# The last head pair of a dilated-attention layer: its softmax shares spread by products, a quarter of its output kept on chip, more PSUM for the projection behind it

## Chip, cores and metric

One core of a Trainium2 chip runs the whole layer as one program. The metric is device time in microseconds (us) of that core, the median over runs of the same program.

## What is computed

The input x has 2048 tokens of 1024 floats. The layer is cut here to what matters:

```python
n = rmsnorm(x) ; proj = n @ w_in                 # split into a GLA group and an attention group
A = gla(...)                                     # 2048 x 512, gated linear attention
for (window, d) in ((128,1), (512,4), (2048,16)):# attention, 8 heads of 64: three branches
    s = masked(q k^T / 8) ; m = max(s) ; den = sum(exp(s - m)) ; o = exp(s - m) v / den
wts = den * exp(m - max over branches of m)
B = sum(wts * o) / sum(wts)                      # 2048 x 512, the branches combined per token and head
h = x + [A ; B] @ w_out
h = h + hier_moe(rmsnorm(h))                     # router: 4 groups of 8 experts, then 2 experts per token
y = rmsnorm(h)
```

A branch's weight over the sum of weights is its *share*; there are three per token and head.

## The kernel before, in words

All data are float32. A product that has to be exact is done as three products of a rounded part (`hi`, fp32r) and a remainder (`lo`): hi*hi, hi*lo, lo*hi. A tile framework puts in the waits, and a scheduler with a model of the engines' times sets the order of instructions on each engine; the source gives priorities by the order in which it emits, and `behind(a, b)` puts a after b.

The stages follow one another: `front` (norm and projection into all columns, with GLA woven in), `att` (lines 495 to 740), `mid` (lines 804 to 969: the attention half of the output projection, second norm, router), and the experts.

**Attention** goes over four pairs of heads, p = 0 to 3, in three branches of 16 query blocks each. `score`, `turn` and `weigh` are its steps, and the unnormalised output of a branch ends in a tile `o` of 128 rows (2 heads x 64) by 2048 tokens. `sums(p)` (line 602) turns the maxima and denominators, writes them to HBM (`stat`) and reads them back in another layout (`nd`, nine transfers, lines 612 to 618), 32 rows (head, block of 128 tokens) by 128 tokens. `shares(p)` (line 620) makes the three shares on VectorE (DVE) with one exponential on ScalarE (ACT), and writes them to HBM (`fac`, line 641). `combine(p, n, eng)` (line 643) handles a quarter n of the tokens, 512: two transfers read `fac` back, each row spread over the 64 rows of a head (`fb`, line 647), then come three multiplications (649), two additions (650, 651), and the result goes to HBM as rows of `oT` (652). For p < 3 all this lies behind the next pair's scores, with the arithmetic on GpSimd (POOL). For p = 3 nothing of attention is left to cover it.

**The GLA half of the output projection** is `out_gla` (line 742), a generator woven into attention: for each of 16 tiles of 128 tokens it turns the GLA output (`og`, line 757, PSUM tile `f`), and does two halves of 512 columns, twelve products each (777 to 779), in a PSUM tile `f` too. The pool `t_fps` has one buffer of that tile. DVE adds x (782), the sum goes to HBM as `hp` (783). `split_wout` (786) makes `hi` on ACT (799) and `lo` on DVE (800) of half the weights, 8 pieces; its second half is called by `mid`.

**mid** loads for each tile of 128 tokens the column block of `oT` (`ot`, 847) and `hp` (`h`, 849), splits `ot` (855, 856), does 24 products in PSUM tiles `mm` (867 to 869, a pool `m_mm` of three buffers), adds `h` (870), norms, and turns the result (894) for the router's products (913). Its products need all of `oT` for their tokens. At the end of the program's attention part, `steps()` runs `sums(3)`, frees the PSUM, sets up `mid`, finishes `out_gla`, makes the shares and combines quarter 0; `build` combines quarters 1 to 3 between mid's first tiles. The experts' weights are prefetched as of mid's third tile, and the experts start when the router's last tile is done.

Of the kernel before, what the change touches and what calls it, by code (L numbers as in the profile page):

```python
# [8 lines left out]
F32 = mybir.dt.float32  # L9
# [4 lines left out]
OP = mybir.AluOpType  # L14
# [3 lines left out]
T = 2048  # L18
# [38 lines left out]
class Layer:  # L57
    def __init__(self, tc, a, scratch):
        self.tc, self.nc, self.a = tc, tc.nc, a
        s = scratch  # L60
        self.gqT = s("gqT", (256, T))
        self.gkT = s("gkT", (256, T))

        self.aq, self.ak = (s(n, (512, T)) for n in ("aq", "ak"))
        self.gv = s("gv", (T, 512))
        self.gs = s("gs", (T, 512))
        self.av = s("av", (4, T, 128))
        self.la_d = s("la_d", (T, 256))
# [3 lines left out]
        self.fac = s("fac", (4, 3, 2 * T))  # L72
# [7 lines left out]
        self.last = None  # L80
        
# [413 lines left out]
    def att(self, gla, left):  # L495
# [83 lines left out]
        def weigh(p, br, blk, kbs, PT):  # L579
            g, b4 = divmod(blk, 4)  # L580
            if blk == 0:
                OU[p, br] = pools["on"].tile([128, T], F32, name=f"o{br}", bufs=2)
# [7 lines left out]
            if b4 == 3:  # L590
                O = OU[p, br]
# [10 lines left out]
        def sums(p):  # L602
# [17 lines left out]
        def shares(p):  # L620
# [19 lines left out]
            nc.vector.tensor_tensor(f[hi], f[hi], mn[hi].unsqueeze(1).broadcast_to((32, 3, 128)), OP.mult)  # L640
            nc.sync.dma_start(self.fac[p].rearrange("b (u m) -> u b m", m=128), f[hi])

        def combine(p, n, eng):
# [4 lines left out]
            for br in range(3):  # L648
                eng.tensor_tensor(fb[:, br], OU[p, br][:, c], fb[:, br], OP.mult)
# [4 lines left out]
        def steps():  # L654
# [81 lines left out]
        return right, lambda n: combine(3, n, nc.vector)  # L736


    def out_gla(self, pools, fps):
# [26 lines left out]
        for i in range(NT):  # L766
# [6 lines left out]
            for f in range(2):  # L773
                fs = slice(f * 512, (f + 1) * 512)
                pp = fps.tile([128, 512], F32, name="f")
                for k in range(4):
                    placed(0, nc.tensor.matmul(pp, oh[:, k, :], woh[:, k, fs], start=k == 0, stop=False))
                    nc.tensor.matmul(pp, oh[:, k, :], wol[:, k, fs], start=False, stop=False)
                    nc.tensor.matmul(pp, ol[:, k, :], woh[:, k, fs], start=False, stop=k == 3)
                    if k < 3:  # L780
                        yield 0.65
# [8 lines left out]
    def split_wout(self, keep, half, raws):  # L790
# [4 lines left out]
        for n in range(8):  # L795
# [4 lines left out]
            nc.vector.tensor_tensor(lo[:, k, c], raw, hi[:, k, c].bitcast(F32), OP.subtract)  # L800
# [5 lines left out]
    def mid(self, st):  # L806
# [6 lines left out]
        mm = pool("m_mm", 3, space=PSUM)  # L813
# [30 lines left out]
        def load(i):  # L844
            rows = slice(i * 128, (i + 1) * 128)
            ot = io.tile([128, 4, 128], F32, name="ot")
            nc.sync.dma_start(ot, self.oT[:, rows].rearrange("(k p) t -> p k t", p=128))
            h = io.tile([128, D], F32, name="h")
            self.loads.append(nc.sync.dma_start(h, self.hp[rows, :]))
            return ot, h  # L850

        def split(ot, h):
            oh = wk.tile([128, 4, 128], F32R, name="oh")
            ol = wk.tile([128, 4, 128], F32R, name="ol")
            nc.scalar.copy(oh, ot)
            nc.vector.tensor_tensor(ol, ot, oh.bitcast(F32), OP.subtract)
# [86 lines left out]
        for i in range(NT + 2):  # L943
            yield
            if i == 2:
# [516 lines left out]
def build(tc, a, scratch, start=None, stop=None):  # L1462
    L = Layer(tc, a, scratch)
    with tc.tile_pool(name="consts", bufs=1) as cp:
# [23 lines left out]
        for i, _ in enumerate(L.mids):  # L1488
            if i < 3:
                last(i + 1)  # L1490
            if i == 2:
# [30 lines left out]
```

## Time and profile before

| | us |
|---|---|
| median of 3 runs | 2243.97 (2239.78 to 2246.97) |
| the profiled execution, its own time | 2231.41 |
| its span, first to last instruction | 2229.7 |
| TensorE (PE) busy | 2080.5 (93%) |
| DVE busy | 1278.7 (57%) |
| ACT busy | 1059.4 (48%) |
| POOL busy | 453.3 (20%) |

The mean granted clock of TensorE is 0.965 of full speed. Engines run side by side, so the busy times add up to more than the span. Times in the rows below are us from the span's start. Attention's last product begins at 1109.11 us, the first product of mid (line 867) at 1154.85, the experts' first (line 1308) at 1328.66.

### The profile page before, as it was taken

Reading aid. Unit: us, or ns where it says so; the run is one execution under the profiler, and the core shown is the slowest. Engines: PE = TensorE matmul, PEld = TensorE weight load, DVE = VectorE, ACT = ScalarE, POOL = GpSimd, SP = SyncE. Lnnn points to the kernel's source line nnn. Section 1 sums busy time; section 2 is a strip of 40 time slices with the busy share of each in tenths; the row PEclk is TensorE's granted clock in tenths of the full one; section 3 lists DMA queues with packets and bytes.
Section 4 is the critical chain, followed back from the end, with each engine's and each line's share of the span. In section 5 each row is a group of like instructions: output and inputs, shape, how many; then the busy total and the mean of one; then the engine's idle time right before and its main releaser. Section 6 shows DMA issues by size and latency. Waiting matters only on the chain. (4 is left out here: it accounts for less than half of the span.)

```text
span 2229.7 us, 38492 instructions
## 1 busy us (share of the span) xinstructions
PE 2080.5 (93%) x15242; PEld 1566.4 (70%) x15242; DVE 1278.7 (57%) x2458; ACT 1059.4 (48%) x1805; POOL 453.3 (20%) x348
## 2 busy tenths in 40 slices
PE   7999999999997999999969978899999999999990
PEld 7799889799885766666647656567766766767760
DVE  5203336424435466666657775666767677767663
ACT  5412335523323366766713333455555555555542
POOL 2000000000002012352300252622212222222246
PEclk9999999999997999999989969999999999999995
DMA  8333333334316415453378727688888888878876
GB/s 252 110 123 101 113 123 110 110 105 128 110 62 202 165 67 143 142 137 95 94 213 297 255 93 251 235 288 302 300 296 283 301 308 312 299 274 291 312 262 235
DMA packets 191465, 440.30 MB, mean 197 GB/s; under 512 B 35201, under 2 KB 107298, under 8 KB 165410
## 3 DMA queue, kind: packets, MB, share of 16 engines
q1 hardware_dynamic: 141842, 351.40, 45.0%
q0 software_dynamic: 21488, 60.36, 10.3%
q10 hardware_dynamic: 27952, 26.05, 4.0%
q8 instruction: 121, 1.98, 0.4%
q14 instruction: 62, 0.51, 0.1%
HBM read 345.89 MB, written 92.40 MB: 197 GB/s over the span
## 5 line engine op out<-in xcount | busy, mean ns | idle before, releaser
L1258 DVE TENSOR_TENSOR lo<-raw,hi 128x2048 fp32r<-128x2048 f32 x192 | 439.4, 2290 | 128.3 <-ACT hi L1258 127.6
L1258 ACT CAST hi<-raw 128x2048 fp32r<-128x2048 f32 x192 | 365.3, 1905 | 208.6 <-DMA raw<-expert_w 195.5
L565 ACT ACTIVATE P<-P,st 128x256 f32<-128x256 f32 (+1 forms) x384 | 174.0, 455 | 96.7 <-DVE st L563 92.2
L214 PE MATMUL mm<-whi,nh 128*128 128x256 f32 x768 | 219.9, 286 | 0.0
L216 PE MATMUL mm<-whi,nl 128*128 128x256 f32 x768 | 218.1, 284 | 0.0
L215 PE MATMUL mm<-wlo,nh 128*128 128x256 f32 x768 | 217.6, 283 | 0.0
L1310 PE MATMUL mm<-lo,nh 128*128 128x512 f32 x512 | 206.8, 405 | 0.0
L1308 PE MATMUL mm<-hi,nh 128*128 128x512 f32 x512 | 204.6, 400 | 1.1 <-ACT nh L1286 1.1
L1309 PE MATMUL mm<-hi,nl 128*128 128x512 f32 x512 | 201.1, 393 | 0.0
L129 POOL TENSOR_TENSOR ss<-ss,mhalf 128x1 f32<-128x1 f32 (+3 forms) x40 | 34.6, 865 | 701.2 <-DVE ss L128 700.9
L563 DVE CUSTOM_DVE_ANT_0 P<-s,amask 128x256 f32<-128x256 f32 (+1 forms) x384 | 124.9, 362 | 66.1 <-PE s L559 42.9
L191 PE MATMUL mm<-nh,whi 128*128 128x512 f32 x384 | 154.5, 402 | 0.0
L192 PE MATMUL mm<-nl,whi 128*128 128x512 f32 x384 | 153.1, 399 | 0.0
L193 PE MATMUL mm<-nh,wlo 128*128 128x512 f32 x384 | 152.7, 398 | 0.0
L214 PEld LDWEIGHTS mm<-whi,nh 128*128 128x128 f32 x768 | 145.4, 189 | 2.0 <-issue 0.7
L215 PEld LDWEIGHTS mm<-wlo,nh 128*128 128x128 f32 x768 | 145.5, 189 | 0.8 <-DVE wlo L177 0.4
L216 PEld LDWEIGHTS mm<-whi,nl 128*128 128x128 f32 x768 | 144.8, 189 | 0.1
L1317 PE MATMUL r<-raw,nr 128*32 128x256 f32 x2048 | 142.9, 383 | 0.0
L559 PE MATMUL s<-k,q 64*128 64x256 f32 (+1 forms) x768 | 132.8, 416 | 0.2 <-DVE st L563 0.2
L1364 POOL DMA_INDIRECT acc<-y,it x32 | 88.7, 2771 | 212.6 <-ACT y L1361 204.9
L1310 PEld LDWEIGHTS mm<-lo,nh 128*128 128x128 f32 x512 | 96.6, 189 | 42.2 <-issue 20.6
L177 DVE TENSOR_TENSOR wlo<-raw,whi 128x1024 fp32r<-128x1024 f32 x48 | 57.0, 1222 | 112.7 <-ACT whi L176 112.7
(326 smaller groups left out, 4147.7 us busy)
## 6 DMA issues: line engine op xcount, KB each, us to landing
raw<-expert_w SPq DMA_DIRECT2D x192, 1024.0 KB, 10.6
raw<-w_in ACTq DMA_DIRECT2D x48, 512.0 KB, 4.9
fb<-fac SPq DMA_DIRECT2D x32, 384.0 KB, 8.4
x<-x SPq DMA_DIRECT2D x16, 512.0 KB, 4.8
og<-og SPq DMA_DIRECT2D x32, 256.0 KB, 4.4
xr<-x SPq DMA_DIRECT2D x32, 256.0 KB, 3.0
v<-av SPq DMA_DIRECT2D x8, 1024.0 KB, 8.1
hp<-xr SPq DMA_DIRECT2D x32, 256.0 KB, 2.3
```

The costliest lines, as they stand in the source:

```text
L191: nc.tensor.matmul(ps, hi[:, k, ms], nh[q][:, k, :], start=k == 0, stop=False)
L192: nc.tensor.matmul(ps, hi[:, k, ms], nl[q][:, k, :], start=False, stop=False)
L193: nc.tensor.matmul(ps, lo[:, k, ms], nh[q][:, k, :], start=False, stop=k == KD - 1)
L214: nc.tensor.matmul(ps[:, j, :], h, hi[:, k, :], start=j == 0 and k == 0, stop=False, skip_group_check=True)
L215: nc.tensor.matmul(ps[:, j, :], h, lo[:, k, :], start=False, stop=False, skip_group_check=True)
L216: nc.tensor.matmul(ps[:, j, :], l, hi[:, k, :], start=False, stop=k == KD - 1, skip_group_check=True)
L565: nc.scalar.activation(P[:, h, 0:w], P[:, h, 0:w], AF.Exp, bias=nm, scale=-1.0, accum_out=dn)
L1258: split = nc.scalar.copy(hi, raw), nc.vector.tensor_tensor(lo, raw, hi.bitcast(F32), OP.subtract)
L1308: nc.tensor.matmul(ps[m], nh[:, k, :], hi[:, kk, :], start=k == 0, stop=False)
L1309: nc.tensor.matmul(ps[m], nl[:, k, :], hi[:, kk, :], start=False, stop=False)
L1310: nc.tensor.matmul(ps[m], nh[:, k, :], lo[:, kk, :], start=False, stop=k == KD - 1)
L1317: nc.tensor.matmul(pr[32 * g:32 * g + 32], nr[:, k, :], raw[:, k % 4, (g % 2) * 256:(g % 2) * 256 + 256], start=k == 0, stop=k == KD - 1, ...
```

## The change

For the last pair only, the shares stay in SBUF (`self.f3`, 32 rows by 3 x 128), and `combine_last` takes the place of `combine`. For each block of 128 tokens two products of a column of the identity (spread to 32 x 64) with the shares copy one row of shares for each head to 64 rows of a PSUM tile of `mm`: 384 columns, plain f32. DVE multiplies the three branches by it straight from PSUM, one instruction of 128 x 384. So there are 2 products and 1 multiplication per block, 32 and 16 in all. The additions of quarter 0 are DVE's, those of quarters 1 to 3 POOL's. Quarter 0 is not written to `oT`: mid's tiles 0 to 3 read it from SBUF (`self.att3`), and split it apart from the other three pairs.

Beside it: the three branches' outputs share one tile; four of the nine `nd` transfers of the last pair are issued by ACT; `lo` of the second half of `w_out` is made on POOL; the second half of each remaining tile of `out_gla` uses a PSUM tile of `mm` once attention is over; `sums` and `shares` are emitted ahead of mid's setup, two tiles of `out_gla` ahead of the combination; quarters 2 and 3 are combined one tile of mid later, as are the experts' first pool and the router's.

```diff
             if b4 == 3:
-                O = OU[p, br]
+                O = OU[p][:, br]
...
+            second = nc.scalar if p == 3 else nc.sync
             for j in range(4):
-                nc.sync.dma_start(nd[j::4, 1].rearrange("g (q i) -> g q i", q=4), src[j])
+                second.dma_start(nd[j::4, 1].rearrange("g (q i) -> g q i", q=4), src[j])
...
+            if p == 3:
+                self.f3 = f
+                return
             nc.sync.dma_start(self.fac[p].rearrange("b (u m) -> u b m", m=128), f[hi])
+
+        def combine_last(n, eng):
+
+            c = slice(n * 512, (n + 1) * 512)
+            fb = pools["sm"].tile([128, 3, 512], F32, name="fb", bufs=2)
+            for b in range(4):
+                blk = 4 * n + b
+                ps = self.mmp.tile([128, 512], F32, name="mm")
+                for h in range(2):
+                    sel = self.ident[32:64, 32 + 16 * h + blk:33 + 16 * h + blk].broadcast_to((32, 64))
+                    mm = nc.tensor.matmul(ps[64 * h:64 * h + 64, 0:384], sel, self.f3[32:64].rearrange("u b m -> u (b m)"),
+                                          start=True, stop=True, skip_group_check=True)
+                    if n == 0:
+                        self.behind(mm, self.outlast, "the factors come later than these products")
+                nc.vector.tensor_tensor(fb[:, :, 128 * b:128 * b + 128], OU[3][:, :, 128 * blk:128 * blk + 128],
+                                        ps[:, 0:384].rearrange("p (b m) -> p b m", b=3), OP.mult)
+            eng.tensor_tensor(fb[:, 0], fb[:, 0], fb[:, 1], OP.add)
+            eng.tensor_tensor(fb[:, 0], fb[:, 0], fb[:, 2], OP.add)
+            if n == 0:
+                self.att3 = fb[:, 0]
+            else:
+                nc.sync.dma_start(self.oT[384:512, c], fb[:, 0])
...
             sums(3)
+            drain(shares(3))
             work.close()
             kst.close()
             self.mids = self.mid(left)
             next(self.mids)
+            weave(out, iter(()), 0, 2)
+            combine_last(0, nc.vector)
             drain(out)
-            sh = shares(3)
-            for _ in range(3):
-                next(sh, None)
-            combine(3, 0, nc.vector)
...
-                pp = fps.tile([128, 512], F32, name="f")
+                pp = fps.tile([128, 512], F32, name="f") if f == 0 or not self.mmp else self.mmp.tile([128, 512], F32, name="mm")
...
-            nc.vector.tensor_tensor(lo[:, k, c], raw, hi[:, k, c].bitcast(F32), OP.subtract)
+            (nc.gpsimd if half else nc.vector).tensor_tensor(lo[:, k, c], raw, hi[:, k, c].bitcast(F32), OP.subtract)
...
+            nk = 3 if i < 4 else 4
+            nc.sync.dma_start(ot[:, 0:nk], self.oT[0:128 * nk, rows].rearrange("(k p) t -> p k t", p=128))
...
+            if i < 4:
+                parts = [(slice(0, 3), ot[:, 0:3]), (slice(3, 4), self.att3[:, i * 128:(i + 1) * 128].unsqueeze(1))]
...
         for i, _ in enumerate(L.mids):
-            if i < 3:
-                last(i + 1)
-            if i == 2:
+
+            for n in {0: (1,), 3: (2, 3)}.get(i, ()):
+                last(n)
+            if i == 3:
                 right.close()
                 L.moe_raw()
```

What stands in a row on an engine changes at three places. Up to attention's last product the order is that of before. The first place is PE between attention and mid; before, the last products of `out_gla` that fall there (`f`) are followed by mid's first (867):

```order
L777 MATMUL f<-woh,oh 128x512
L778 MATMUL f<-wol,oh 128x512
L779 MATMUL f<-woh,ol 128x512
L867 MATMUL mm<-woh,oh 128x512
L868 MATMUL mm<-wol,oh 128x512
```

Of the change, the first of quarter 0's products (655) and, further on, the end of the stretch:

```order
L801 MATMUL f<-woh,oh 128x512
L802 MATMUL f<-wol,oh 128x512
L803 MATMUL f<-woh,ol 128x512
L655 MATMUL mm<-f,ident 64x384 x6
L781 MATMUL f<-ident,og 128x128 x4
L655 MATMUL mm<-f,ident 64x384 x2
L801 MATMUL mm<-woh,oh 128x512
```

Quarter 0 stands behind half a tile of `out_gla`, in the same row on PE. The end of the stretch, with quarter 1's last copies and mid's first products (897 to 899):

```order
L801 MATMUL mm<-woh,oh 128x512
L802 MATMUL mm<-wol,oh 128x512
L803 MATMUL mm<-woh,ol 128x512
L655 MATMUL mm<-f,ident 64x384 x4
L897 MATMUL mm<-woh,oh 128x512
```

Before, 72 of the 108 products of `out_gla` that attention left over stood ahead of mid's first product, and 36 among mid's first tiles. Now all 108 stand ahead, 48 of them before the first 655 rows and 60 behind, and so do 16 of the 32 copying products.

The second place is DVE, in the second half of the shares (638 to 640, `f` at the end is the shares). Before:

```order
L782 TENSOR_TENSOR xr<-f,xr 128x512
L638 TENSOR_TENSOR mn<-nd 32x128
L800 TENSOR_TENSOR wol<-xr,woh 128x512
L638 TENSOR_TENSOR mn<-mn,nd 32x128
L800 TENSOR_TENSOR wol<-xr,woh 128x512
L639 RECIPROCAL mn<-mn 32x128
L800 TENSOR_TENSOR wol<-xr,woh 128x512
L835 CAST tri<-trf 128x128
L761 TENSOR_TENSOR ol<-f,oh 128x512
L800 TENSOR_TENSOR wol<-xr,woh 128x512
L640 TENSOR_TENSOR f<-f,mn 32x384
```

Of the `lo` pieces of `w_out` (800) four stand among the shares. The same part of DVE's row in the change (785 and 806 are `out_gla`'s):

```order
L806 TENSOR_TENSOR xr<-mm,xr 128x512
L859 CAST tri<-trf 128x128
L638 TENSOR_TENSOR mn<-nd 32x128
L785 TENSOR_TENSOR ol<-f,oh 128x512
L638 TENSOR_TENSOR mn<-mn,nd 32x128
L639 RECIPROCAL mn<-mn 32x128
L640 TENSOR_TENSOR f<-f,mn 32x384
L806 TENSOR_TENSOR xr<-f,xr 128x512
L659 TENSOR_TENSOR fb<-o,mm 128x3x128 x4
```

They have left the row; all eight stand in a row on POOL now. Behind the shares come quarter 0's four multiplications (659), with no transfer between.

The third place is PE in mid, between the last product of tile 2 and the first of tile 3 (924 turns a tile for the router, 943 and 948 are the router's). Before, a tile's turning stood among products of the next tile, or of `out_gla`:

```order
L868 MATMUL mm<-wol,oh 128x512
L869 MATMUL mm<-woh,ol 128x512
L894 MATMUL tp<-ident,n_11426 128x128 x8
L867 MATMUL mm<-woh,oh 128x512
L868 MATMUL mm<-wol,oh 128x512
```

Nothing but a tile's turning parts the products there. Of the change, at the end of tile 2:

```order
L899 MATMUL mm<-woh,ol 128x512
L655 MATMUL mm<-f,ident 64x384 x2
L924 MATMUL tp<-ident,n_11435 128x128 x8
L655 MATMUL mm<-f,ident 64x384 x6
L943 MATMUL sm<-nT,rw 64x256 x8
L655 MATMUL mm<-f,ident 64x384 x2
L924 MATMUL tp<-ident,n_11497 128x128 x8
L655 MATMUL mm<-f,ident 64x384 x4
L948 MATMUL sm<-ident,lT 128x128 x2
L655 MATMUL mm<-f,ident 64x384 x2
L897 MATMUL mm<-woh,oh 128x512
```

Quarters 2 and 3 are copied here, 16 products in one place, and tile 2's own turning now stands ahead of tile 3's products.

## Rows read from the trace of the kernel before

**Rows 1.** Busy time by stretch: us, engines busy (instructions), clock share, DMA share, GB/s
```profile
1109.70:1154.85 45.15, 25.97 (x87) 18.90 (x85) 22.27 (x40) 8.20 (x14) 0.00 (x0) 0.77 0.69 201
1154.85:1301.40 146.55, 139.35 (x742) 106.53 (x740) 102.52 (x293) 49.89 (x123) 25.67 (x32) 0.98 0.80 256
```

**Rows 2.** Waits of PE, 1109 to 1180 us: total, times, longest
```profile
PE f L777 <- DVE ol L761: 11.9, 3, 6.5
PE f L777 <- DVE xr L782: 4.5, 3, 2.7
```

**Rows 3.** Timeline of PE: start, us, line, out<-in, count, idle before and releaser
```profile
1109.70 0.66 PE L757 MATMUL f<-ident,og 128*128 128x128 f32 x4
1111.76 0.50 PE L777 MATMUL f<-woh,oh 128*128 128x512 f32 x1 [1.40 <-DVE ol L761]
...
1125.42 0.79 PE L777 MATMUL f<-woh,oh 128*128 128x512 f32 x1 [4.04 <-DVE ol L761]
...
1130.27 0.44 PE L779 MATMUL f<-woh,ol 128*128 128x512 f32 x1
1131.59 0.47 PE L777 MATMUL f<-woh,oh 128*128 128x512 f32 x1 [0.88 <-DVE xr L782]
...
1134.17 0.39 PE L779 MATMUL f<-woh,ol 128*128 128x512 f32 x1
...
1142.47 0.80 PE L777 MATMUL f<-woh,oh 128*128 128x512 f32 x1 [6.47 <-DVE ol L761]
...
1154.85 0.40 PE L867 MATMUL mm<-woh,oh 128*128 128x512 f32 x1
```

**Rows 4.** Timeline of DVE, the shares and the first combination
```profile
1115.86 0.39 DVE L628 TENSOR_TENSOR mn<-nd 32x128 f32<-32x128 f32 x1 [0.29 <-DMA nd<-stat]
...
1121.11 0.69 DVE L800 TENSOR_TENSOR wol<-xr,woh 128x512 fp32r<-128x512 f32 x1
...
1125.99 0.55 DVE L640 TENSOR_TENSOR f<-f,mn 32x384 f32<-32x384 f32 x1
...
1139.91 1.90 DVE L649 TENSOR_TENSOR fb<-o,fb 128x512 f32<-128x512 f32 x3 [4.63 <-DMA fb<-fac]
...
1145.87 1.90 DVE L649 TENSOR_TENSOR fb<-o,fb 128x512 f32<-128x512 f32 x3 [2.86 <-DMA fb<-fac]
```

**Rows 5.** Timeline of SP's queue (issues), then of ACT
```profile
1109.61 0.33 SPq L609 DMA_DIRECT2D stat<-sb  x1
...
1114.48 2.06 SPq L618 DMA_DIRECT2D nd<-stat  x4
...
1132.01 1.92 SPq L647 DMA_DIRECT2D fb<-fac  x3
...
1150.52 0.37 SPq L847 DMA_DIRECT2D ot<-oT  x1
...
1153.69 0.62 ACT L855 CAST oh<-ot 128x512 fp32r<-128x512 f32 x1 [17.02 <-DMA ot<-oT]
```

**Rows 6.** Timeline of PE in mid: plain f32 products, then the next instruction
```profile
1293.36 1.95 PE L913 MATMUL sm<-nT,rw 128*64 128x256 f32 x16
1295.24 0.50 PE L869 MATMUL mm<-woh,ol 128*128 128x512 f32 x1
```

**Rows 7.** Instructions of lines 649 and 870: ns min/median/max, first and last start
```profile
L649 POOL TENSOR_TENSOR fb<-o,fb x36: 1261/1276/1301, 876.7 to 1079.2; 128x512 f32<-128x512 f32 x36
...
L649 DVE TENSOR_TENSOR fb<-o,fb x12: 684/686/693, 1139.9 to 1170.6; 128x512 f32<-128x512 f32 x12
...
L870 DVE TENSOR_TENSOR h<-mm,h x32: 680/686/709, 1163.8 to 1297.5; 128x512 f32<-128x512 f32 x32
```

**Rows 8.** Timelines of POOL and of DVE among the experts
```profile
1413.92 0.96 POOL L1186 DMA_INDIRECT perm<-tok,pos  x1 [0.30 <-issue]
1415.19 3.04 POOL L1186 DMA_INDIRECT perm<-tok,pos  x1 [0.30 <-issue]
...
1415.10 2.29 DVE L1258 TENSOR_TENSOR lo<-raw,hi 128x2048 fp32r<-128x2048 f32 x1 [1.48 <-ACT hi L1258]
```

**Rows 9.** Waits of PE, 1180 to 1300 us
```profile
PE mm L867 <- DVE h L870: 4.7, 1, 4.7
```

More of the change, by code (lines that the diff above doesn't have):

```diff
@@ L71, in __init__ @@
         self.stat = s("stat", (4, 192, 128))
-        self.fac = s("fac", (4, 3, 2 * T))
+        self.fac = s("fac", (3, 3, 2 * T))
         self.oT = s("oT", (512, T))
@@ L79, in __init__ @@
         self.entries, self.loads = [], []
-        self.last = None
+        self.last = self.mmp = None
     def pool(self, st, name, bufs, **k):
@@ L580, in weigh @@
             g, b4 = divmod(blk, 4)
-            if blk == 0:
-                OU[p, br] = pools["on"].tile([128, T], F32, name=f"o{br}", bufs=2)
+            if (br, blk) == (0, 0):
+                OU[p] = pools["on"].tile([128, 3, T], F32, name="o", bufs=2)
             if b4 == 0:
@@ L648, in combine @@
             for br in range(3):
-                eng.tensor_tensor(fb[:, br], OU[p, br][:, c], fb[:, br], OP.mult)
+                eng.tensor_tensor(fb[:, br], OU[p][:, br, c], fb[:, br], OP.mult)
             eng.tensor_tensor(fb[:, 0], fb[:, 0], fb[:, 1], OP.add)
@@ L735, in att @@
         drain(steps(), out)
-        return right, lambda n: combine(3, n, nc.vector)
+        return right, lambda n: combine_last(n, nc.gpsimd)
     def out_gla(self, pools, fps):
@@ L778, in out_gla @@
                     nc.tensor.matmul(pp, oh[:, k, :], wol[:, k, fs], start=False, stop=False)
-                    nc.tensor.matmul(pp, ol[:, k, :], woh[:, k, fs], start=False, stop=k == 3)
+                    self.outlast = nc.tensor.matmul(pp, ol[:, k, :], woh[:, k, fs], start=False, stop=k == 3)
                     if k < 3:
@@ L812, in mid @@
         wk = pool("m_wk", 2)
-        mm = pool("m_mm", 3, space=PSUM)
+        mm = self.mmp = pool("m_mm", 3, space=PSUM)
         tps = pool("m_tps", 2, space=PSUM)
@@ L846, in load, with split @@
             ot = io.tile([128, 4, 128], F32, name="ot")
-            nc.sync.dma_start(ot, self.oT[:, rows].rearrange("(k p) t -> p k t", p=128))
+            nk = 3 if i < 4 else 4
+            nc.sync.dma_start(ot[:, 0:nk], self.oT[0:128 * nk, rows].rearrange("(k p) t -> p k t", p=128))
             h = io.tile([128, D], F32, name="h")
             self.loads.append(nc.sync.dma_start(h, self.hp[rows, :]))
-            return ot, h
-        def split(ot, h):
+            return i, ot, h
+        def split(i, ot, h):
             oh = wk.tile([128, 4, 128], F32R, name="oh")
             ol = wk.tile([128, 4, 128], F32R, name="ol")
-            nc.scalar.copy(oh, ot)
-            nc.vector.tensor_tensor(ol, ot, oh.bitcast(F32), OP.subtract)
+            parts = [(slice(0, 4), ot)]
+            if i < 4:
+                parts = [(slice(0, 3), ot[:, 0:3]), (slice(3, 4), self.att3[:, i * 128:(i + 1) * 128].unsqueeze(1))]
+            for c, t in parts:
+                nc.scalar.copy(oh[:, c], t)
+                nc.vector.tensor_tensor(ol[:, c], t, oh[:, c].bitcast(F32), OP.subtract)
             return oh, ol, h
@@ L1488, in build @@
         for i, _ in enumerate(L.mids):
-            if i < 3:
-                last(i + 1)
-            if i == 2:
+            for n in {0: (1,), 3: (2, 3)}.get(i, ()):
+                last(n)
+            if i == 3:
                 right.close()
```

## Prediction

> **What bounds the kernel now.** I read the timeline of PE first, for the place the change touches. Attention's last products end about 1109.7 us, and the middle stage's first product comes at 1154.85 [rows 3]. In those 45.15 us PE is busy for 25.97 by the page, at a mean granted clock of 0.77, while in the 146.55 us behind it is busy for 139.35 at 0.98 [rows 1]. So the stretch ahead of the middle stage is a hole, and the middle stage is bound by PE. The work that PE has in the hole is 72 products of the GLA projection and three turnings. At 2.4 GHz twelve products run from 1131.59 to the twelfth's start at 1134.17, 0.235 us each, and a turning takes 0.66 [rows 3]. That is 72 x 0.235 + 3 x 0.66 = 18.9 us, and the loss is **26.2 us**.
>
> Where the loss goes is in two views. The waits of PE give 11.9 us for `ol`, the split of a turned tile, and 4.5 for the sum with x that frees the one PSUM buffer [rows 2]. The rest is clock: from 1125.42 to 1130.27 twelve products start 0.44 us apart, the lower level of 1.2 GHz, behind an idle stretch of 4.04 us [rows 3].
>
> What sets the hole's length is a chain that is not PE's. The timelines of DVE, SP and ACT [rows 4, 5] show it: maxima and denominators go out at 1109.61, the last of nine reads is issued up to 1116.54, DVE makes the shares from 1115.86 to 1126.54, writes them, waits 4.63 us for the spread rows, combines, writes `oT`, and ACT, idle for 17.02 us, splits the first `ot` at 1153.69. From the shares' end to mid's first product are 28.3 us; DVE's own work in them for quarter 0 is five instructions of 0.686 [rows 7]. The GLA products that would fill PE stand in an order whose waits this chain delays too: the products at 1142.47 waited 6.47 us for `ol`, because DVE had quarter 0's multiplications ahead of it, which themselves waited 4.63 us for the spread rows [rows 3, 4].
>
> **The change, part by part.** *Removed:* the write of the shares, the eight reads that spread them, quarter 0's write and its part of four reads. They were the chain. What is late next is PE's own queue: all 108 remaining GLA products now stand ahead of mid's first. The 36 that move forward leave mid, so they are neutral in the sum. The hole becomes 108 products, 25.4 us, with turnings, copies and what stalls are left.
>
> *Stalls left in the hole.* (a) A turning needs ACT's and DVE's split before its products: 1.40 us in the shortest case, 4.04 in the longer one [rows 3]. Of three such places, the order fills two with products of another half-tile, which the PSUM of `mm` makes possible. I take 2.5 for the one left. (b) The first copying products wait for the shares, and everything behind them on PE waits too. Before, the shares were done at 1126.54, with four pieces of `lo` of 0.69 among them [rows 4]. Without these 2.8 us, and with four of the reads on ACT's queue, of which the last four took 2.06 us on SP [rows 5], they would be done between 1122 and 1124. PE gets there after 48 products, a turning and (a): 1109.7 + 0.7 + 48 x 0.235 + 0.7 + 2.5 = 1124.9. I take 1 us, between 0 and 5. (c) Clock: before, some 33 products ran at 1.2 GHz, 0.2 us more each, 6.6 us. With shorter idle stretches I take 2, between 0 and 6.6. (d) The fourth block waits for a PSUM buffer, and each turning for DVE's sum with x: 2 us, from three waits of 0.7, which is one DVE instruction from PSUM [rows 7]. Together 7.5, so the hole gives back 26.2 - 7.5 = **18.7 us**.
>
> *Added on PE:* 32 copying products of 384 columns. The nearest rows are the router's plain f32 products, which also fill 64 rows of the output in pairs: 16 of 256 columns take 1.88 us to the next instruction, 0.235 a pair [rows 6]. For 384 columns that is 0.35, and 16 pairs cost **5.6 us**. From below: nothing, if they only fill waits. From above: a turning's product of 128 columns is 0.66 / 4 = 0.165, so 384 columns alone are 0.5, and 1.0 at the lower clock: 15.8 to 31.7 us. I take the pairs, since row and column shapes are nearest.
>
> *Added on DVE:* 16 multiplications of 384 columns from PSUM, 0.51 us each by three quarters of line 870's 0.686 [rows 7]. Against them 12 multiplications and 6 additions of 0.686 and 8 pieces of `lo` go, so DVE loses work: nothing in the sum. POOL gains 8 pieces of `lo` and 6 additions of 1.28 us, 18 us, where it was idle. Its powers for the second norm queue behind four of these additions, 5.1 us, but one tile of mid takes longer (24 x 0.235 = 5.6), so nothing.
>
> *In mid:* the copies for quarters 2 and 3 stand in one place on PE, with a turning behind that needs the tile just finished. Eight multiplications on DVE are 4.1 us, and three PSUM buffers let PE run three blocks ahead; the turnings and router products between fill most of it. PE's wait: 0 if they fill all, 8 if DVE's norm of the tile and the multiplications come one after another without cover. I take **2 us**.
>
> *Transfers:* SP's row loses fourteen issues: the shares' write, eight reads, quarter 0's write, and four reads that ACT issues now. Those four wait on ACT until `stat`, issued at 1109.61, is written; the first reads were with DVE by 1115.86 [rows 4, 5]. Behind them on ACT stand the casts of `w_out`, which mid needs only at its first product, and the exponential of the shares, which needs these reads anyway: nothing. The experts' weights are issued at the same tiles of mid as before, so they arrive earlier by what mid starts earlier; behind mid nothing is touched.
>
> The sum: 18.7 - 5.6 - 2 = **11.1 us** off. The profiled execution's 2231.41 would become 2220.3. The runs' median, 2243.97, stands 12.6 us above that execution, and I take the difference off the median: **2232.9 us**.
>
> **The rivals.** *More is gained.* Mid has a wait of 4.7 us of PE for `h` [rows 9], which may shift or go with less traffic in front; if it goes and the stalls left are 4 instead of 7.5, the gain is 26.2 - 4 - 5.6 - 2 + 4.7 = 19.3 us: 2224.7. For it: the DMA share of the hole drops. Against: every stall has to go at once.
>
> *The shares wait for POOL.* All eight pieces of `lo` are on POOL, 1.28 us each, just while DVE makes the shares from two inputs in SBUF each. The trace shows such a pair interfere, among the experts: a POOL issue of 0.96 us takes 3.04 beside DVE's `lo`, an instruction with two SBUF inputs, and ends 0.94 after DVE does [rows 8]. The trace has no row in which POOL holds up DVE. If each piece holds up the shares once, they are 8 x 1.28 = 10.2 us later; 2 of these are PE's slack, 1 is in the sum, and about 7 come on top, since the GLA products stand behind the copies on PE: gain 4, 2240. The Trainium skill, page "SBUF — State Buffer", section "Who interferes with whom", says that a DVE instruction with two SBUF inputs and a GpSimd instruction that reads SBUF exclude each other for the whole instruction, whichever came first. By that rule this rival is the case; the trace agrees for a POOL issue that waits, and no row here shows the other direction. Against the full price: POOL gets its pieces two at a time as the weights land.
>
> *The copies cost more than the hole gives.* If the copying products don't overlap in pairs and half of them run at the lower clock, 32 cost 23.7 us in place of 5.6: 18.7 - 23.7 - 2 = 7 us slower, 2251. It decides at 0.52 us a product; above 0.73 the kernel is slower by over 0.3%. For it: each waits for DVE in a row that nothing can overtake. Against: the router's rows [rows 6].
>
> *The hole is not the chain's.* If PE's own waits on DVE set the pace for all 108 products as they did before (16.4 us of waits for 72 of them), the loss stays at some 22 of the 26.2 us and the copies come on top: 26.2 - 22 - 5.6 - 2 is 3 us slower, 2247, no change. For it: the waits of the GLA products are the largest named item [rows 2]. Against: most of them follow the chain.
>
> **How the numbers follow.** What a measurement of this kernel can tell from no change is about 0.3%, 6.7 us. Chances: the forecast, a gain of 7 to 15 us, 0.46; more, 0.21; POOL in the way, 0.19; the hole stays, 0.05; the copies too dear, 0.09. So faster 0.67, same 0.24, slower 0.09. The range reaches from a gain of 22 us, 2222, to no gain, 2244; outside lie the last rival, part of the fourth and the scatter of the runs (7 us from lowest to highest).
>
> **What would show it.** Right, if mid's first product comes some 38 us after attention's end in place of 45 (28 of GLA products and turnings, 2.8 of copies, 7.5 of stalls), with all 108 GLA products ahead of it; if pairs of copies take about 0.35 us; if PE's waits for `ol` drop below 5 us and ACT's 17 us wait for `ot` is gone; if mid's last product and the experts' first move forward by 10 to 12 us, and the experts take as long as before. Wrong, if the shares end later than 1126 (POOL), if copies stand at 0.5 us or more, if PE idles among the copies of quarters 2 and 3 by more than 4 us, or if the experts start no earlier though mid does.

## The result and the profile after

The changed kernel takes 2226.25 us, the median of five runs (2223.29 to 2228.16); beside it the kernel before took 2240.67 (2239.78 to 2246.97). The ratio is 0.9927, with a 95% interval of 0.991 to 0.9943: 14.4 us less. The forecast was 2232.9, a gain of 11.1 us; of the 6.7 us between the two times 3.3 are the median of before, which five runs put at 2240.67 in place of 2243.97.

The profiled execution after takes 2223.29 us, with a span of 2221.3 and a granted clock of 0.967. The windows by stage are attention's last turning to the middle stage's first product (the hole), from there to the experts' first product, and the rest. They answer to [rows 1]; the columns are those of [rows 1].

```profile
1108.38:1149.66 41.28, 35.77 (x158) 25.21 (x156) 22.99 (x39) 9.32 (x18) 10.55 (x8) 0.92 0.62 199
1149.66:1316.60 166.94, 147.03 (x809) 111.09 (x807) 116.16 (x383) 61.20 (x135) 47.93 (x50) 0.90 0.65 218
1316.60:2221.30 904.70, 829.00 (x5892) 578.95 (x5892) 600.25 (x467) 474.57 (x379) 268.95 (x166) 0.95 0.81 281
```

The hole is 41.28 us in place of 45.15, though it now holds 108 GLA products in place of 72, and 16 copying products. PE is busy for 35.77 of it, at a clock of 0.92 in place of 0.77.

The waits of PE from 1105 to 1316 us, which answer to [rows 2, 9] (the lines between them are waits of the router's and the experts' products):

```profile
PE f L801 <- DVE ol L785: 4.7, 1, 4.7
...
PE mm L801 <- ACT oh L784: 0.7, 1, 0.7
PE tp L924 <- DVE n L912: 0.6, 1, 0.6
```

Of the 16.4 us of waits of the GLA products 5.4 are left, and the 4.7 us wait for `h` is gone. Now the timeline of PE, beside [rows 3] (start, us, line, what, count, idle before and releaser):

```profile
1108.38 0.66 PE L781 MATMUL f<-ident,og 128*128 128x128 f32 x4
...
1117.43 0.60 PE L781 MATMUL f<-ident,og 128*128 128x128 f32 x4
1122.72 0.79 PE L801 MATMUL f<-woh,oh 128*128 128x512 f32 x1 [4.69 <-DVE ol L785]
1123.31 0.63 PE L802 MATMUL f<-wol,oh 128*128 128x512 f32 x1
...
1127.86 2.15 PE L655 MATMUL mm<-f,ident 32*64 32x384 f32 x12
1129.94 0.66 PE L781 MATMUL f<-ident,og 128*128 128x128 f32 x4
1130.53 0.86 PE L655 MATMUL mm<-f,ident 32*64 32x384 f32 x4
1131.32 0.50 PE L801 MATMUL mm<-woh,oh 128*128 128x512 f32 x1
...
1149.66 0.50 PE L897 MATMUL mm<-woh,oh 128*128 128x512 f32 x1
```

One turning is still exposed, for 4.69 us, with eleven of the next twelve products at the lower clock, as [rows 3] has it at 1125.42. And the copies: where the order of instructions has six products the trace has twelve rows (x12), and they take 2.08 us. **A plain f32 product is two rows on PE**, called two passes from here on (a turning, four products in four rows, is not); a product of 384 columns costs 0.35 us, a block of two 0.70.

DVE's shares, beside [rows 4], and POOL in the same time:

```profile
1114.29 0.76 DVE L628 TENSOR_TENSOR mn<-nd 32x128 f32<-32x128 f32 x1 [1.41 <-DMA nd<-stat]
1115.09 1.38 DVE L629 TENSOR_TENSOR mn<-mn,nd 32x128 f32<-32x128 f32 x1
...
1120.60 1.34 DVE L638 TENSOR_TENSOR mn<-nd 32x128 f32<-32x128 f32 x1
1121.97 0.69 DVE L785 TENSOR_TENSOR ol<-f,oh 128x512 fp32r<-128x512 f32 x1
...
1124.34 0.55 DVE L640 TENSOR_TENSOR f<-f,mn 32x384 f32<-32x384 f32 x1
```

```profile
1113.52 2.70 POOL L824 TENSOR_TENSOR wol<-xr,woh 128x512 fp32r<-128x512 f32 x2 [29.27 <-ACT woh L823]
1119.16 5.31 POOL L824 TENSOR_TENSOR wol<-xr,woh 128x512 fp32r<-128x512 f32 x4 [2.95 <-ACT woh L823]
```

The shares end 16.5 us after attention's last turning (1124.89 less 1108.38), as before (1126.54 less 1109.70 is 16.8): four pieces of `lo` have left DVE's row, but instructions that took 0.39 us take 0.76, 1.38 and 1.34 while POOL makes them.

### The profile page after: what moved, and what is told of

Same layout as the page of the kernel before. It is cut to its first block, busy times and chain, and to the rows that moved or that the text cites. A ratio compares the mean times of both kernels' runs of the same rounds, so it can differ in the third digit from the quotient of the medians.

```text
span 2221.3 us, 38624 instructions
## 1 busy us (share of the span) xinstructions
PE 2086.3 (94%) x15306; PEld 1567.7 (71%) x15306; DVE 1272.1 (57%) x2452; ACT 1060.2 (48%) x1809; POOL 474.5 (21%) x362
## 5 line engine op out<-in xcount | busy, mean ns | idle before, releaser
L1394 POOL DMA_INDIRECT acc<-y,it x32 | 93.9, 2934 | 228.7 <-ACT y L1391 222.5
```

## The experiments

All times of stages are counted from attention's last turning (T). The scatter between executions of one program is in the first five rows; the ratios are to the runs of the kernel before beside each. e8 and e9 each differ from e7 by the edit named.

| run | median us | ratio (95%) | T to middle | middle | T to experts | experts to end |
|---|---|---|---|---|---|---|
| before | | | 45.2 | 173.8 | 219.0 | 901.0 |
| b1, before again | 2235.73 (one) | | 45.1 | 172.1 | 217.3 | 907.7 |
| b2, before again | 2245.71 (one) | | 45.5 | 176.8 | 222.3 | 911.4 |
| after | 2226.25 | 0.9927 (0.991 to 0.9943) | 41.3 | 166.9 | 208.2 | 904.7 |
| a1, after again | 2224.37 | 0.993 (0.9906 to 0.9954) | 44.7 | 165.1 | 209.8 | 903.0 |
| e1, `lo` on DVE | 2223.25 | 0.9926 (0.9902 to 0.9949) | 40.8 | 163.8 | 204.7 | 908.0 |
| e2, one PSUM buffer | 2226.56 | 0.9938 (0.9913 to 0.9962) | 30.0 | 181.5 | 211.4 | 904.6 |
| e3, shares by HBM | 2234.66 | 0.9971 (0.996 to 0.9983) | 46.0 | 171.9 | 217.8 | 903.0 |
| e4, copies twice | 2253.05 | 1.0037 (1.002 to 1.0054) | 53.1 | 180.4 | 233.5 | 911.1 |
| e5, one copy of 128 rows | 2226.9 | 0.9944 (0.9922 to 0.9966) | 44.9 | 167.0 | 212.0 | 904.0 |
| e7, rounded copies | 2220.88 | 0.9905 (0.9885 to 0.9926) | 41.1 | 165.8 | 206.8 | 907.9 |
| e8, e7 with `lo` on DVE | 2220.5 | 0.9907 (0.9886 to 0.9928) | 40.3 | 162.4 | 202.6 | 906.9 |
| e9, e7 with turnings in `mm` | 2221.54 | 0.9908 (0.9886 to 0.993) | 39.0 | 165.2 | 204.2 | 903.6 |
| e10, quarters earlier | 2231.11 | 0.9952 (0.9936 to 0.9967) | 45.2 | 171.7 | 216.9 | 904.9 |

### Both kernels again

> The kernel before once more, for a second profile. Question: the two profiled executions differ by 8.1 us where the medians differ by 14.4; the experts took 901.0 us before (1328.66 to 2229.7) and 904.7 after. Theory (scatter): the experts of this execution take 901 to 906 us, hole 45 +- 1 us, the middle stage without its 36 GLA products 164 to 165. Rival (the change makes the experts slower): the experts take 901 +- 1 here and 904.7 +- 1 in the repeat of the changed kernel.

> The kernel before a third time, for its profile. The stretch from attention's last turning to the experts' first product was 219.0 and 217.3 us before, 208.2 and 209.8 after: 9.1 less, while the medians differ by 14 to 15; from the experts' first product to their sixth group it was 152.6 and 160.3 before, 158.0 and 155.2 after. Theory (scatter of the experts' start): 217 to 220 and anything from 152 to 162, the two adding up to the time by themselves. Rival (the change also gains among the experts): 160 or more here.

> The changed kernel once more, timed beside the experiments. Theory: 0.993 of before (0.991 to 0.995); in its profile the hole from attention's last turning to the middle stage's first product is 41 +- 1 us, the 32 copies take 0.35 us a product, the middle stage 161 +- 1 without copies, the experts as long as in the repeat of before within 1 us. Rival: the experts 3 to 4 us longer than before's again, which would make the gain of the changed region 14 us less 3.5.

From T to the experts the three profiles of before take 219.5 us on average, the two of after 209.0: **10.5 us** of the gain lie there. The experts take 901.0, 907.7 and 911.4 us before, which is one and the same program, and 904.7 and 903.0 after. So the 8.1 us between the first profiles of the two kernels understate the gain because that execution of before had the shortest experts' stage of the three. Several figures lie outside what was expected: the experts in b1 (907.7 for 901 to 906), the stretch from T in b2 (222.3 for 217 to 220), and of a1 the middle stage without copies (159.2 for 160 to 162), the experts (903.0, where b1's 907.7 were to be met within 1 us) and the hole (44.7 for 42 at most). From the experts' first product to their sixth group b2 took 162.6 us, which is on the side of the rival that the change also gains there; with 152.6, 160.3 and 162.6 before and 158.0 and 155.2 after, that stays open. What made a1's hole longer is the next thing that the trace shows. Its PE timeline, and two windows of it:

```profile
1129.36 2.15 PE L655 MATMUL mm<-f,ident 32*64 32x384 f32 x12
1131.44 0.66 PE L781 MATMUL f<-ident,og 128*128 128x128 f32 x4
1132.03 0.86 PE L655 MATMUL mm<-f,ident 32*64 32x384 f32 x4
1132.82 0.79 PE L801 MATMUL mm<-woh,oh 128*128 128x512 f32 x1
1133.41 0.63 PE L802 MATMUL mm<-wol,oh 128*128 128x512 f32 x1
```

```profile
1129.36:1131.44 2.08, 2.08 (x14) 0.75 (x13) 1.77 (x3) 0.29 (x1) 1.27 (x1) 1.00 1.02 389
1132.82:1135.97 3.15, 3.15 (x9) 2.48 (x8) 2.83 (x5) 0.54 (x2) 0.00 (x0) 0.50 0.28 109
```

The granted clock falls to 0.50 (1.2 GHz) right behind the copies, while PE is busy for all of both windows. It happens once more behind the next copies, at 1146.43. The 15 GLA products in the two stretches start 0.43 us apart in place of 0.23, 3.0 us in sum, which is most of the 3.4 between the two holes. In the first profile of after the clock stayed up behind the copies of the hole. e10, whose edit leaves the hole's order as it is, has 15 products at the lower clock behind the same copies again, and e1 eight. So the copies have a second price, which differs from run to run, and the first profile of after is the exception among these four.

### Copies twice (e4)

```diff
+                    nc.tensor.matmul(ps[64 * h:64 * h + 64, 0:384], sel, self.f3[32:64].rearrange("u b m -> u (b m)"),
+                                     start=True, stop=True, skip_group_check=True)
                     mm = nc.tensor.matmul(ps[64 * h:64 * h + 64, 0:384], sel, self.f3[32:64].rearrange("u b m -> u (b m)"),
```

> The changed kernel with each of the 32 copying products issued twice into the same PSUM rows (same values, no other work). Theory (a copying product is two passes on PE, 0.35 us by the trace, on the path): 32 x 0.35 = 11.2 us slower than the changed kernel, 5.6 of it ahead of the middle stage's first product and 5.6 in that stage; about 0.998 of before. Rival A (the two halves of a block overlap, 0.175 us a product): 5.6 us slower. Rival B (the copies lie in PE's waits): under 3 us slower.

It is 24 us slower than the changed kernel (1.0037 against 0.993 of some 2241), twice what was expected. The timeline of PE at the end of quarters 2 and 3 (L655 and L657 are the two copies, L899 and L900 the middle stage), and two windows there:

```profile
1192.02 0.86 PE L655 MATMUL mm<-f,ident 32*64 32x384 f32 x4
...
1195.58 1.55 PE L655 MATMUL mm<-f,ident 32*64 32x384 f32 x4
...
1201.55 0.63 PE L900 MATMUL mm<-wol,oh 128*128 128x512 f32 x1
```

```profile
1192.67:1200.95 8.28, 8.28 (x29) 3.40 (x25) 1.26 (x3) 1.17 (x2) 1.45 (x2) 0.52 0.49 160
1200.95:1206.60 5.65, 5.65 (x15) 4.46 (x14) 0.68 (x2) 0.00 (x0) 2.55 (x2) 0.50 0.12 46
```

For 13.9 us PE never idles, and the clock is at its lower level; the copies themselves then take twice as long (1.55 for 0.86), and 13 products behind them start 0.43 apart. Over the whole kernel, by the timeline, copies take 28.1 us in place of 11.6, 16.5 more, and 38 products of 512 columns lie at the lower clock, 7.6 us: 24.1 together. The theory's 11.2 for the passes fits, and the clock came on top. The twelve runs of e4 spread widely: two, of 2238.51 and 2240.71 us at a mean clock of 0.966 and 0.965, lie 12 to 16 us above the changed kernel's two medians, not far from the price of the passes alone; the other ten lie at 2246.76 to 2256.36, the profiled one at 2255.07 with a mean clock of 0.962. More copies, more time at 1.2 GHz, with no idle ahead of it: that copies bring the clock down is shown; why some groups do and others don't is not.

### One copy of 128 rows (e5)

```diff
-                for h in range(2):
-                    sel = self.ident[32:64, 32 + 16 * h + blk:33 + 16 * h + blk].broadcast_to((32, 64))
-                    mm = nc.tensor.matmul(ps[64 * h:64 * h + 64, 0:384], sel, self.f3[32:64].rearrange("u b m -> u (b m)"),
...
+                mm = nc.tensor.matmul(ps[:, 0:384], pick[b // 3][32:64, b % 3], self.f3[32:64].rearrange("u b m -> u (b m)"),
...
```

`pick` holds the stationary operands, 32 rows by 128 columns for a block.

> The changed kernel with one copying product per block, whose stationary operand picks both heads' rows for 128 rows of PSUM, in place of two of 64 rows: 16 products for 32, and two short ACT copies per quarter that make the stationary operands in buffers that are free by then. Theory (a product costs its 0.35 us whatever rows it fills, on the path): 16 x 0.35 = 5.6 us faster than the changed kernel (0.9905 of before). Rival A (a product that fills 128 rows takes twice as long): no change. Rival B (ACT's copies come late, the products wait): no gain in the hole, 2.8 in the middle stage.

Rival A it is. Three products of 128 rows, six passes, take as long as six of 64 rows did:

```profile
1127.38 2.21 PE L657 MATMUL mm<-f,nd 32*128 32x384 f32 x6
1129.52 0.66 PE L783 MATMUL f<-ident,og 128*128 128x128 f32 x4
```

That is 2.14 / 3 = 0.71 us a block, as after (0.70), and no gain. A pass of 128 rows takes 0.36 us. That two products of 64 rows run side by side, and don't merely take half as long each, the starts in e4 show: a pass of each copy (L655 and L657) starts at 1184.05, and again at 1185.34. The prediction's pairs exist, but a block is two such pairs, not one.

### Rounded copies (e7)

```diff
-                self.f3 = f
+                self.f3 = pools["sm"].tile([64, 3, 128], F32R, name="nd", bufs=1)
+                nc.scalar.copy(self.f3[hi], f[hi])
+                nc.vector.tensor_tensor(self.f3[lo], f[hi], self.f3[hi].bitcast(F32), OP.subtract)
...
-                    mm = nc.tensor.matmul(ps[64 * h:64 * h + 64, 0:384], sel, self.f3[32:64].rearrange("u b m -> u (b m)"),
+                mm = nc.tensor.matmul(ps[:, 0:384], pick[b // 3][0:64, b % 3], self.f3.rearrange("u b m -> u (b m)"),
...
```

> The changed kernel with the shares split into a rounded part and a remainder (fp32r, 32 rows each, stacked to 64), and one product per block that adds both while it spreads them to 128 rows: 16 products of 128 x 384 for 32 of two passes. ACT makes the rounded part and the stationary operands, DVE the remainder. Theory (a plain f32 product is two passes, and such copies also lower the clock behind them): a rounded product of 512 columns takes 0.235 us, so 384 take 0.18; 16 of them 2.8 us in place of 11.2, and no lower clock right behind them, which cost 3 us in one of two profiles: 8 to 11 us faster than the changed kernel, 0.989 of before. Rival A (the price lies in the 384 columns to PSUM or in DVE's multiplications, whatever the product): within 2 us. Rival B (rounding and operands make the first copies late): gain of 4 to 6, with a wait of PE at the first copy of 1.5 us or more.

Quarter 0's last block with the products behind it, two blocks at the upper clock, and a wait from the middle stage:

```profile
1129.72 0.44 PE L660 MATMUL mm<-nd,sb 64*128 64x384 f32 x1 [0.37 <-DVE fb L664]
1130.18 0.76 PE L806 MATMUL mm<-woh,oh 128*128 128x512 f32 x1
1130.73 0.63 PE L807 MATMUL mm<-wol,oh 128*128 128x512 f32 x1
...
1142.01 0.61 PE L660 MATMUL mm<-nd,f 64*128 64x384 f32 x2
1142.56 0.50 PE L806 MATMUL f<-woh,oh 128*128 128x512 f32 x1
```

```profile
PE mm L902 <- DVE h L905: 2.5, 1, 2.5
```

A block falls from 0.70 to 0.28 us, and all copies from 11.6 to 5.3 by the timeline, waits among them included. Of these 6.3 us only 2.2 are seen from T to the experts (206.8 against 209.0), and the medians differ by 3.5 to 5.4. PE now waits for DVE where the copies used to cover it: 0.4 for a multiplication of quarter 0, 0.8 for a sum with x ahead of a turning, 2.5 for `h`. It is less than the 8 to 11 expected, and "no lower clock right behind them" did not hold: behind quarter 0's copies, around which PE also waited 1.2 us, eight products run at the lower level (from 1130.18), in e8 as well; in e9 none do. Up to the start of the stage's last product e7 takes 172.8 us from T, after 169.3 and a1 172.0; the 2.2 us lie behind it, among the router's last products, where the clock differs from run to run (see e1 below). That the medians' gain comes from the cheaper copies is therefore likely but not shown by the stages.

### `lo` back on DVE (e1), and with the rounded copies (e8)

```diff
-            (nc.gpsimd if half else nc.vector).tensor_tensor(lo[:, k, c], raw, hi[:, k, c].bitcast(F32), OP.subtract)
+            nc.vector.tensor_tensor(lo[:, k, c], raw, hi[:, k, c].bitcast(F32), OP.subtract)
```

> The changed kernel with the eight pieces of lo of the second half of w_out back on DVE. Theory (the lock between POOL and DVE costs about what the pieces cost in DVE's row): DVE's instructions of the shares fall from 0.76, 1.38, 0.58, 1.34 and 0.63 us to about 0.4 each, 2.9 us back, while some four pieces of 0.69 come into the row; the shares end within 1 us of where they end now, and the time is within 3 us (0.15%) of the changed kernel. Rival A (the lock is the dearer one): shares 2 to 3 us earlier, 2 to 3 us faster. Rival B (DVE's row is the dearer one, the shift of lo is part of the gain): shares and the splits of turned tiles 3 us or more later, 3 to 6 us slower.

And of e8, where "the one before" is e7:

> The one before, with the eight pieces of lo of w_out's second half on DVE again. Theory (POOL's lock and DVE's row cost the same): within 2 us of the one before. Rival (the wait for ol, 4.7 us with lo on POOL and 3.2 with it on DVE, is on the path): 1.5 to 3 us faster.

DVE in e1:

```profile
1113.92 0.39 DVE L628 TENSOR_TENSOR mn<-nd 32x128 f32<-32x128 f32 x1
...
1115.55 0.40 DVE L629 TENSOR_TENSOR mn<-mn,nd 32x128 f32<-32x128 f32 x1
...
1121.49 0.39 DVE L638 TENSOR_TENSOR mn<-nd 32x128 f32<-32x128 f32 x1
...
1124.76 0.55 DVE L640 TENSOR_TENSOR f<-f,mn 32x384 f32<-32x384 f32 x1
```

With POOL idle the same instructions take 0.39, 0.40 and 0.39: that POOL's pieces hold DVE up is shown. The shares end 17.3 us after T, 0.8 later than after, and the times are within 1.1 us (e1) and 0.4 us (e8) of their partners. So the lock costs about what the pieces cost in DVE's row, and the move of `lo` brings nothing. PE's wait for `ol` falls from 4.7 to 3.2 us, and in the single profiles of e1 and e8 T to the experts is some 4 us shorter; the medians show none of it. In e1 that is not the wait: its last product of the middle stage starts 170.5 us after T, after's 169.3. The difference lies behind it, in the same 58 instructions of PE that end the router's work, first in after, then in e1 (columns as in [rows 1]):

```profile
1284.41:1294.66 10.25, 10.25 (x58) 9.70 (x56) 4.48 (x16) 1.26 (x3) 0.00 (x0) 0.50 0.16 65
1284.43:1290.84 6.41, 6.36 (x58) 5.83 (x56) 4.21 (x16) 1.26 (x3) 0.00 (x0) 1.00 0.26 103
```

They take 10.25 us at the lower clock and 6.41 at the upper one, and the experts start 3.6 us earlier from T. a1's last products of the router are at the lower clock too for the most part.

### Shares through HBM (e3)

```diff
             if p == 3:
-                self.f3 = f
-                return
...
-            combine_last(0, nc.vector)
+            combine(3, 0, nc.vector)
...
-        return right, lambda n: combine_last(n, nc.gpsimd)
+        return right, lambda n: combine(3, n, nc.vector)
...
-            nk = 3 if i < 4 else 4
+            nk = 4
...
```

> The changed kernel with the last pair's shares written to HBM and read back spread, as before, the four quarters combined on DVE and all read from oT; no copying products. PSUM, lo on POOL, the four reads on ACT and the order of emission stay as changed. From the rows: the shares end 16.5 us after attention's last turning, and before it took 28.3 us from there to the middle stage's first product, so that product comes some 45 us after the turning (41.3 and 44.7 in the two profiles of the changed kernel); the 108 GLA products are done after some 35, PE idles about 10 us, and the middle stage is without its 16 copies (5.6 us). Theory A (the chain through HBM is worth what the copies cost, no more; most of the gain is that the GLA products fill the chain): from the turning to the experts 207 to 211 us, time within 3 us of the changed kernel. Rival B (the chain through HBM is what the change gained by): the first product at 48 us or later, time 5 to 12 us above the changed kernel, near that of before.

The time is rival B's, 9 us above the changed kernel, though the hole is theory A's: 46.0 us, with PE idle for 9.9. In its place the middle stage was longer than either had it, 171.9 where 160 follow from after's without its copies. PE's timeline at its first product (L894), and its waits from 1105 to 1326 us:

```profile
1154.46 0.79 PE L894 MATMUL mm<-woh,oh 128*128 128x512 f32 x1 [9.89 <-ACT oh L882]
1155.06 0.63 PE L895 MATMUL mm<-wol,oh 128*128 128x512 f32 x1
```

```profile
PE mm L894 <- DVE h L897: 6.2, 2, 3.6
```

Nine products behind the idle stretch are at the lower clock (1.8 us), and two waits for `h`, 6.2 us, stand in the stage, with lower clock behind them. So keeping the shares and quarter 0 on the chip, with the additions of quarters 1 to 3 on POOL, is worth 9 of the 14 to 15 us, copies and their clock paid for, and by the stages (46.0 against 43.0, 171.9 against 166.0) two thirds of it are won behind the hole.

### One PSUM buffer (e2), quarters earlier (e10), turnings in `mm` (e9)

```diff
-                pp = fps.tile([128, 512], F32, name="f") if f == 0 or not self.mmp else self.mmp.tile([128, 512], F32, name="mm")
+                pp = fps.tile([128, 512], F32, name="f")
```

> The changed kernel with out_gla's second halves back in the one PSUM buffer f; the copies and everything else stay. Theory (the second buffer is what closes the stalls): the scheduler's order lets GLA products lie among the middle stage's again, PE waits for the sum with x (0.7 to 2.7 us each) and for ol come back in the hole, and the time is 4 to 9 us above the changed kernel (about 0.996 of before). Rival (the transfers that went are all of it): the products only change places, within 2 us of the changed kernel.

60 GLA products go back among the middle stage's, as the theory had it, but T to the experts is only 2.4 us longer than after, and the ratio 0.0008 higher, less than its interval. The measured 2 us are below the 4 to 9 expected, and can't be told from nothing, nor from 4.

```diff
-            if i == 3:
+            if i == 2:
                 rt = self.pool(st, "m_rt", 2, side="right")
...
-            for n in {0: (1,), 3: (2, 3)}.get(i, ()):
-                last(n)
-            if i == 3:
+            if i < 3:
+                last(i + 1)
+            if i == 2:
```

> The changed kernel with quarters 2 and 3, the experts' first pool and the router's one tile of the middle stage earlier, as before. The middle stage took 3.3 us less after the change than its instructions' count said, where a wait of 2 us more was forecast, and PE's wait of 4.7 us for h was gone. Theory (by the later place the copies lie beside turnings and router products, and SP's queue is clear of the experts' loads when h is wanted): 2 to 5 us slower than the changed kernel, and a wait for h or for a PSUM buffer shows in the middle stage. Rival (the wait for h was in the products of the GLA half that lay there, or scatter): within 1.5 us.

It is 5 to 7 us slower than the changed kernel by the medians, and the middle stage 5.7 longer (171.7 against 166.0). PE in it:

```profile
1159.21 2.85 PE L655 MATMUL mm<-f,ident 32*64 32x384 f32 x16
1161.99 0.50 PE L897 MATMUL mm<-woh,oh 128*128 128x512 f32 x1
...
1163.14 0.63 PE L898 MATMUL mm<-wol,oh 128*128 128x512 f32 x1
...
1255.04 0.80 PE L897 MATMUL mm<-woh,oh 128*128 128x512 f32 x1 [2.08 <-DVE h L900]
```

Sixteen passes of copies among the stage's products bring the clock down for nine products (1.8 us), and the wait for `h` is back, 2.1 us with eight products at the lower clock behind it (1.6): 5.5 together. In after and a1, by the later place, neither is there. The place alone does not explain the wait: e7, e8 and e9 have the later place and wait 2.4 to 2.5 us for `h`, e3, which has no copies, 6.2. It is absent only where plain f32 copies stand at the later place.

```diff
-            t = fps.tile([128, 4, 128], F32, name="f")
+            t = fps.tile([128, 4, 128], F32, name="f") if not self.mmp else self.mmp.tile([128, 4, 128], F32, name="mm")
```

e9 is made from e7, with `lo` on POOL: "the one before" of its text is e7.

> The one before, with out_gla's turnings in a PSUM buffer of mm once attention is over, so that a turning can stand a half-tile earlier on PE. Theory (the split of a turned tile is late because its turning waits for the one buffer f): the wait for ol (3.2 us or more) and the lower clock of the twelve products behind it (12 x 0.2 = 2.4) go, 3 to 6 us faster than the one before. Rival (three buffers of mm are too few for turnings, half-tiles and copies together): waits for DVE's sums and multiplications in their place, no gain.

The rival is right. The turning stands earlier, but in place of e7's wait of 4.7 us for `ol` PE waits 2.3 for it, 1.5 for `oh` and 2.1 for a sum with x; the mean clock of the hole is 0.96 in place of 0.88, yet the time is that of e7 within 0.7 us. (Its T is the first turning too, which here starts 0.7 us later behind attention.) The rounded copies are the fastest form that ran, 0.9905 to 0.9908 in three versions, some 5 us below the changed kernel; the intervals overlap.

## Why the prediction came out, step by step

- **Bound and direction: right.** The hole was the chain's. ACT's 17.02 us wait for `ot` [rows 5] is gone, all 108 products stand ahead of the middle stage, and with the chain put back (e3) 9 us of the gain go and PE idles for 9.9 us.
- **Stalls left, 7.5 us: right in sum in one profile of two, not in its parts.** 108 products, four turnings and the copies are 25.4 + 2.6 + 5.7; of 41.28 us that leaves 7.5. The exposed turning cost 4.7 in place of 2.5, and nothing of the waits for shares or PSUM was there; the clock took 2.1. The second profile had 10.9, by the clock behind copies.
- **The copies, "16 pairs cost 5.6 us": the term that failed.** The step was reading the 16 rows of [rows 6] as 16 products; they are eight of two passes. Measured: 0.70 us a block and 11.6 in all, double the term; the sign "pairs of copies take about 0.35 us" failed with it. The bounds (0 to 31.7) held it, and at 0.35 us a product it stayed below the 0.52 at which the third rival decides. That a copy can lower the clock of the products behind it had no term at all: 0 and 3.0 us in the hole of two profiles, and 3.0 again in e10's.
- **"In mid: PE's wait, I take 2 us": wrong in sign.** Without GLA products, their turning (9.1 us) and copies the stage took 165.1 us before on average, and takes 160.2: 4.9 less in place of 2 more. Turnings and router products between the copies hide all of DVE's multiplications, and the wait of 4.7 for `h` [rows 9], which the first rival named, is gone with the lower clock behind it. The later place of the quarters has a part in that (e10), and so has the copies' own time, since the wait is back where they are cheaper (e7) or left out (e3): the two terms are not independent. To the start of the stage's last product the gain from T is 13.8 us (184.4 to 170.7 on average); the router's tail gives back 3.3 of them (35.1 to 38.4 us), where more of its products now stand behind that product.
- **The sum.** 18.7 - 5.6 - 2 was the forecast. By stage, on the means of three profiles before and two after, it was 17.2 (26.4 lost before, less the 9.2 that 7.5 and 10.9 make on average) - 11.6 + 4.9 = 10.5, the 10.5 between the profiles. Two wrong terms of nearly equal size cancelled, so the nearness of 11.1 owes something to luck. The medians' 14.4 has 3 to 4 more, in the experts' stage, whose scatter from 901 to 911 in one program is larger than that; that the change gains there is open.
- **The rival on POOL: its mechanism was right, its price not.** DVE's instructions stretch from 0.39 to 1.38 us beside POOL's pieces, so that the trace now has the direction that [rows 8] lacked (in those rows POOL's issue ends 0.84 us after DVE's instruction, not 0.94). The Trainium skill, "SBUF — State Buffer", "Who interferes with whom", says that such a pair excludes each other; this trace agrees. But as e1 shows, it took back only what the pieces had cost DVE.

## What to carry to other kernels

Count the rows that a product leaves in the trace against the order of instructions before a price is taken from them: a plain f32 product is two passes, so spreading rows by products is paid twice, and a rounded part plus a remainder stacked in one fp32r product is cheaper. Put such thin products beside other small work, not in a row among large ones, since the clock behind them is part of their price. When a stall is removed, ask what the freed engine waits for next: here copies cheaper by 6.3 us gave 2 to 5. Before a difference between two profiles is put down to an edit, compare the granted clock of like stretches: e1's 4 us were 58 instructions behind the edit's place.

## What was not expected of the hardware

- The granted clock fell to its lower level with PE busy without a break: 3.15 of 3.15 us at 0.50 behind copies in a1, 13.9 us at 0.50 to 0.52 in e4, 10.25 of 10.25 at 0.50 among after's last router products. What brings the clock down in these places no run shows. The Trainium skill, "TensorE: Matmul & The Clock Gate", "HAM oscillation — how this bites in real kernels", speaks of idle gaps; by that rule the clock would have stayed up here, and the trace does not agree.
- The same copying products, 2.08 us for the first six each time, were followed by a fall in a1 and by none in after; the same 58 router instructions ran at 0.50 in after and at 1.00 in e1.
- Two f32 products of 64 rows take as long as one of 128 rows, 0.70 against 0.71 us.
